# Angle tables of a state-space layer as products of two short tables, built for one pair of groups at a time

## The chip, the cores and the metric

The kernel runs on one core of one Trainium2 chip. The metric is the device time of one execution in microseconds. The three runs of the kernel before took 2749.91, 2758.4 and 2762.81 us, so its median is 2758.4 us.

## The reference

The program is one layer of a hybrid encoder over 2048 positions and 1024 channels. One normalized input h goes through one input projection whose columns feed three head groups: a diagonal complex state-space layer (S5), a differential attention and an HGRN2 gated recurrence. Their outputs go through one output projection and are added to the input; a gated MLP with a causal convolution and a last normalization follow. The change lies wholly in the first group:

```python
dt = exp(log_step)[:, None]
mag, ang = exp(lam_re * dt), lam_im * dt          # 16 groups x 64 states
lb = mag * (cos(ang) + i sin(ang))
bu[s] = B_bar @ u[s]                               # per group, 16 inputs
x[s]  = lb * x[s-1] + bu[s]                        # complex scan over 2048 positions
y     = Re(C @ x) + d * u
out   = gelu(y) * sigmoid(gelu(y) @ w_glu)
```

## The kernel before

`phase_s5` computes the layer with the 2048 positions cut into 256 chunks of T = 8. Inside a chunk the recurrence is folded into matrices (QP, QS, MG, C1, C2). Between chunks only the state after each chunk is scanned, 256 steps per group. To make that scan real, each state is turned back by its angle times the chunk number, scanned with the real factor `mag8`, and turned forward again. This takes a cosine and a sine table of 256 entries for each of the 16 groups on each of 128 partitions: the tiles `s_ct` and `s_sn`.

The phase has two parts, and both are Python generators whose `yield` marks where other work may be emitted between.

The parameter part (lines 383 to 552) runs beside the first normalization and projection (`phase_a`). It makes `E`, the sine and cosine of the angle times 8, 16, ... 1024 (line 478), QP and QS by rotations on VectorE (lines 516 to 519), and C1 and C2 by the same rotation on GpSimd, eight times six instructions (line 536, written in the body of the lambda at line 537). The rotations take their temporaries from the pool `s_e`, tags `t0` and `t1`, two buffers each. The pool is closed at line 553, and the pool `s_w` of the main part is opened after it on the same side of the memory.

The main part (lines 556 to 669) loops over four quarters `q` of four groups each. A quarter loads its inputs `U` by two DMAs on the queue of SyncE (line 560; the tile has two buffers). It then builds `CT` and `SN` for its four groups on GpSimd, one buffer each, by doubling: in step i the first n = 2^i columns, turned by E[i], give the next n columns, with six instructions a step (lines 577 to 584) and eight steps. Then come two pairs of groups. For a pair, ScalarE copies `s_un` out of U, TensorE transposes it (`s_pu`, line 594) and QP and QS (`s_pq`, line 604), TensorE multiplies (`s_pw`, line 617), VectorE multiplies the result by the two tables (`s_w`, lines 623 and 624), GpSimd adds (line 625), VectorE scans (`s_yy`, line 627), GpSimd multiplies by the two tables (`s_ya`, `s_yb`, lines 633 and 636), and TensorE sums three products (`s_py`, lines 646 to 651) for the gelu. The five PSUM tiles of this part share three buffers of one tag.

Beside the main part run the rest of the input projection (`a_p`) and the preparation of MLP weights (`f_sum`, `f_w`, `Wd`), which are the left side of a weave; the right side is S5, then HGRN2 (`phase_hgrn`), then output projection and MLP (`phase_tail`). After the projections the left side becomes the attention. The weave fixes the order in which work is emitted, by costs attached to the yields (6.0 for a projection step, 5.0 for an S5 step, 2.5 for an HGRN2 step). A planner then lists the instructions of each engine in a fixed order, and on the chip each engine runs its list in order and waits for what its next instruction needs.

Of the kernel before, what the change touches and what calls it, by code (L numbers as in the profile page):

```python
# [9 lines left out]
F32 = mybir.dt.float32  # L10
# [4 lines left out]
ALU = mybir.AluOpType  # L15
# [342 lines left out]
def phase_s5(K, Ud, lam_re, lam_im, log_step, b_re, b_im, c_re, c_im, d, w_glu, Yd):  # L358


    tc, nc = K.tc, K.nc
    G, N, P, T, C = 16, 64, 16, 8, 256
    V = nc.vector

    def b3(a, n):
        return a.rearrange("p (g o) -> p g o", o=1).to_broadcast([128, a.shape[1], n])

    with ExitStack() as es:
# [4 lines left out]
        with ExitStack() as e2:  # L373
            cp = e2.enter_context(tc.tile_pool(name="s_c", bufs=1, reuse_waits="tile", side="right"))
            e3 = ExitStack()
            wk = e3.enter_context(tc.tile_pool(name="s_e", bufs=2, reuse_waits="tile", side="right"))
# [10 lines left out]
            for i, dst in enumerate((re, im)):  # L387
# [8 lines left out]
                out=ls, in_=log_step[0].rearrange("(o g) -> o g", o=1).to_broadcast([128, G])  # L396
# [23 lines left out]
            def tt(o, a, b, op):  # L420
                V.tensor_tensor(out=o, in0=a, in1=b, op=op)
# [25 lines left out]
            c1 = 6.28125  # L447
# [90 lines left out]

            MG = cp.tile([128, T, G, P], F32, name="s_mg")
# [15 lines left out]
            wk = e2.enter_context(tc.tile_pool(name="s_w", bufs=2, reuse_waits="tile", side="right"))  # L555
            for q in range(4):
                gs = slice(4 * q, 4 * q + 4)
                U = wk.tile([128, 2, T, 64], F32, tag="u", name="s_u")
# [6 lines left out]
                CT = wk.tile([128, 4, C], F32, tag="ct", bufs=1, name="s_ct")  # L565
                SN = wk.tile([128, 4, C], F32, tag="sn", bufs=1, name="s_sn")
                nc.gpsimd.memset(CT[:, :, 0:1], 1.0)
                nc.gpsimd.memset(SN[:, :, 0:1], 0.0)
                for i in range(8):
                    n = 1 << i  # L570
                    sw, co = E[i]
                    sb, cb = b3(sw[:, gs], n), b3(co[:, gs], n)
                    a, b = CT[:, :, 0:n], SN[:, :, 0:n]
                    t0 = wk.tile([128, 4, 128], F32, tag="tb0", bufs=1, name="s_tb0")
                    t1 = wk.tile([128, 4, 128], F32, tag="tb1", bufs=1, name="s_tb1")
                    pt = nc.gpsimd.tensor_tensor
                    pt(out=t0[:, :, 0:n], in0=a, in1=cb, op=ALU.mult)
                    pt(out=t1[:, :, 0:n], in0=b, in1=sb, op=ALU.mult)
                    pt(out=CT[:, :, n:2 * n], in0=t0[:, :, 0:n], in1=t1[:, :, 0:n], op=ALU.subtract)
                    t0 = wk.tile([128, 4, 128], F32, tag="tb0", bufs=1, name="s_tb0")  # L580
                    t1 = wk.tile([128, 4, 128], F32, tag="tb1", bufs=1, name="s_tb1")
                    pt(out=t0[:, :, 0:n], in0=b, in1=cb, op=ALU.mult)
                    pt(out=t1[:, :, 0:n], in0=a, in1=sb, op=ALU.mult)
                    pt(out=SN[:, :, n:2 * n], in0=t0[:, :, 0:n], in1=t1[:, :, 0:n], op=ALU.add)
                yield 1
                for gg in range(0, 4, 2):
                    UG = wk.tile([128, 2, C], F32, tag="ug", name="s_ug")
# [24 lines left out]
                    for e in range(2):  # L612
                        g = 4 * q + gg + e
                        l = gg + e
                        pw = ps_p.tile([128, 2, C], F32, tag="s", name="s_pw")
                        for i in range(2):
# [6 lines left out]
                        tt(w0, pw[:, 0, :], CT[:, l, :], ALU.mult)  # L623
                        tt(w1, pw[:, 1, :], SN[:, l, :], ALU.mult)
# [9 lines left out]
                            out=YA[:, e, 1:C], in0=yy[:, 0:C - 1], in1=CT[:, l, 0:C - 1], op=ALU.mult  # L634
                        )
                        nc.gpsimd.tensor_tensor(
                            out=YB[:, e, 1:C], in0=yy[:, 0:C - 1], in1=SN[:, l, 0:C - 1], op=ALU.mult
# [1497 lines left out]
```

## Time and profile before

| | |
|---|---|
| median of three runs | 2758.4 us |
| profiled execution, device time | 2750.61 us |
| its span | 2748.9 us |
| TensorE busy | 2429.6 us (88%) |
| VectorE busy | 1924.5 us (70%) |
| GpSimd busy | 1357.3 us (49%) |
| granted TensorE clock, mean | 0.928 |

The span runs from the first to the last instruction of the profiled execution; the device time has 1.7 us around it. TensorE is the busiest engine, so a stretch in which it stands idle is the first place where time can be won. Busy shares of the whole say little of one stage: GpSimd is at 49% over the span, and far above that while S5 runs.

### The profile page before, as it was taken

The numbers are of one execution on the slowest core, as the hardware profiler recorded it, in microseconds if no ns is written. First come the engines' busy times: TensorE is split into PE (matmuls) and PEld (weight loads), VectorE is DVE, ScalarE is ACT, GpSimd is POOL, SyncE is SP. The second block draws the span as 40 slices with busy tenths as digits, with TensorE's granted clock in tenths as the row PEclk, the third lists the DMA queues.
The fourth block names the chain that finished last, engine by engine and source line by source line (L and its number), as shares of the span: only waits on it lengthen the run. The fifth ranks groups of instructions, "written<-read, shape, count | busy, mean of one in ns | idle before, by whom it ended". The sixth has DMA issues, their size and how long they took to land. (4 is left out here: it accounts for less than half of the span.)

```text
span 2748.9 us, 42509 instructions
## 1 busy us (share of the span) xinstructions
PE 2429.6 (88%) x15438; PEld 1365.9 (50%) x15438; DVE 1924.5 (70%) x3497; ACT 1255.9 (46%) x2270; POOL 1357.3 (49%) x1149
## 2 busy tenths in 40 slices
PE   5998888988988899759998888599989999999998
PEld 4655547767766665334443334244435444444444
DVE  7567746888888785698678998966464655455565
ACT  6333344666656453465446566533144433333221
POOL 5788602444534442267656866615232444444280
PEclk8999999999988878869999999799999999999999
DMA  7675555565665446655555566598785655554733
GB/s 242 234 222 196 172 159 120 117 139 121 112 142 126 92 116 180 165 132 146 180 174 150 168 165 173 185 285 260 256 285 184 219 158 150 162 157 138 282 97 123
DMA packets 556738, 473.06 MB, mean 172 GB/s; under 512 B 277296, under 2 KB 433264, under 8 KB 555504
## 3 DMA queue, kind: packets, MB, share of 16 engines
q1 hardware_dynamic: 534352, 429.97, 55.1%
q10 hardware_dynamic: 22176, 40.38, 4.0%
q8 instruction: 121, 1.98, 0.3%
q14 instruction: 89, 0.73, 0.1%
HBM read 290.35 MB, written 125.83 MB: 151 GB/s over the span
## 5 line engine op out<-in xcount | busy, mean ns | idle before, releaser
L96 PE MATMUL f_pm<-f_q,f_w 128*128 128x512 f16 x3696 | 839.2, 387 | 34.5 <-DVE f_u L1863 10.4
L96 PEld LDWEIGHTS <-f_w 128*128 128x128 f16 x3696 | 363.6, 99 | 502.7 <-issue 77.0
L1786 PE MATMUL f_pd<-f_dw,f_da 128*128 128x512 f16 x1848 | 411.0, 384 | 8.4 <-DVE f_r L1764 7.0
L891 POOL TENSOR_TENSOR t_sc<-t_sc 128x1024 f16<-128x1024 f32 (+7 forms) x144 | 256.8, 1796 | 274.4 <-ACT t_sc L890 247.1
L1786 PEld LDWEIGHTS <-f_da 128*128 128x128 f16 x1848 | 182.0, 99 | 231.5 <-issue 21.5
L848 ACT ACTIVATE t_sc<-t_sc,t_nm 128x128 f32<-128x128 f32 (+7 forms) x192 | 228.9, 1194 | 81.6 <-DVE t_nm L843 81.0
L832 PE MATMUL t_ps<-t_k,t_q 96*128 96x512 f16 (+2 forms) x480 | 168.9, 386 | 100.6 <-DVE t_mx L836 93.3
L836 DVE CUSTOM_DVE_ANT_0 t_sc<-t_ps,t_base,t_mx 128x512 f32<-128x512 f32 (+3 forms) x288 | 185.2, 644 | 24.7 <-PE t_ps L832 15.5
L61 DVE TENSOR_TENSOR f_a<-f_t,f_a 128x512 f16<-128x512 f32 x132 | 155.6, 1200 | 53.4 <-ACT f_a L55 53.0
L867 DVE SCALAR_TENSOR_TENSOR t_sc<-t_sc,t_a 128x1024 f32<-128x1024 f32 (+7 forms) x144 | 180.5, 1279 | 1.3
L96 PE MATMUL g_pv<-g_w,g_h 128*128 128x256 f16 x1152 | 154.3, 292 | 18.7 <-ACT g_w L55 11.8
L913 PEld LDWEIGHTS <-t_wt 128*128 128x128 f16 x2448 | 108.2, 104 | 110.2 <-DMA t_wt<-t_sc 49.2
L1863 POOL TENSOR_TENSOR f_t<-f_t,f_t 128x512 f32<-128x512 f32 x66 | 100.9, 1543 | 121.2 <-ACT f_a L55 109.8
L96 PE MATMUL g_pq<-g_h,g_w 128*128 128x256 f16 x1152 | 149.7, 288 | 10.4 <-DVE g_sg L1160 5.4
L913 PE MATMUL t_po<-t_v,t_wt 128*128 128x64 f16 x2448 | 121.5, 202 | 38.3 <-DMA t_wt<-t_sc 33.0
L1863 POOL TENSOR_TENSOR f_k<-f_k,f_k 128x512 f32<-128x512 f32 x88 | 124.7, 1417 | 59.3 <-ACT f_k L1895 26.0
L1617 DVE SCALAR_TENSOR_TENSOR f_t<-f_u,f_cw,f_t 128x1024 f32<-128x1024 f32 x88 | 125.5, 1426 | 32.5 <-ACT f_t L1615 31.7
L890 ACT CAST t_sc<-t_sc 128x1024 f16<-128x1024 f32 (+7 forms) x144 | 111.7, 792 | 77.9 <-DVE t_sc L867 73.6
L836 DVE CUSTOM_DVE_ANT_0 t_sc<-t_ps,t_base 128x512 f32<-128x512 f32 (+2 forms) x192 | 121.0, 633 | 34.8 <-PE t_ps L832 21.4
L96 PEld LDWEIGHTS <-g_h 128*128 128x128 f16 x1152 | 118.0, 104 | 50.6 <-issue 22.5
L55 ACT ACTIVATE f_a<-f_t 128x512 f16<-128x512 f32 x154 | 94.8, 627 | 96.4 <-DVE f_a L61 32.1
L55 ACT ACTIVATE f_w<-f_sum 128x512 f16<-128x512 f32 x110 | 69.1, 628 | 150.0 <-DVE f_sum L139 65.1
(335 smaller groups left out, 4490.0 us busy)
## 6 DMA issues: line engine op xcount, KB each, us to landing
f_w<-Wd SPq DMA_DIRECT2D x231, 256.0 KB, 3.0
Wd<-f_w SPq DMA_DIRECT2D x154, 256.0 KB, 2.1
Ad<-f_a ACTq DMA_DIRECT2D x154, 256.0 KB, 2.6
f_da<-Ad SPq DMA_DIRECT2D x42, 768.0 KB, 5.1
g_h<-Hd SPq DMA_DIRECT2D x24, 1024.0 KB, 6.7
f_dst<-in_w_down_dram SPq DMA_DIRECT2D x48, 512.0 KB, 4.6
o_wst<-in_w_out_dram SPq DMA_DIRECT2D x24, 512.0 KB, 5.5
f_wst<-in_w_gate_dram SPq DMA_DIRECT2D x22, 512.0 KB, 5.5
```

The lines of the kernel that those rows point to most:

```text
L55: nc.scalar.activation(out=hi, in_=src, func=AF.Copy, scale=scale)
L61: nc.vector.tensor_tensor(out=lo, in0=src, in1=hi, op=ALU.subtract)
L96: nc.tensor.matmul(out=out, lhsT=lhs(a, k), rhs=rhs(b, k), start=(n == 0), stop=(n == 3 * nk - 1))
L832: nc.tensor.matmul(out=ps[:, 0:k1 - k0], lhsT=qt[:, c, 128 * (i % 4):128 * (i % 4) + 128], rhs=H.k[:, c, k0:k1], start=True, stop=True,)
L836: V.tensor_tensor_reduce(out=sc[c][:, k0:k1], in0=ps[:, 0:k1 - k0], in1=bs[:, k0:k1], scale=1.0, scalar=-3e38 if j == 0 else mx[:, c, j - ...
L848: nc.scalar.activation(out=sc[c][:, 0:L], in_=sc[c][:, 0:L], func=AF.Exp, scale=SLOPES[h], bias=nm[:, c:c + 1], accum_out=H.la[:, c, n_:n_ ...
L867: V.scalar_tensor_tensor(out=sc[0][:, k0:k1], in0=sc[1][:, k0:k1], scalar=a[:, 1:2], in1=sc[0][:, k0:k1], op0=ALU.mult, op1=ALU.add,)
L891: nc.gpsimd.tensor_tensor(out=hl[:, LM + k0:LM + k1], in0=sc[0][:, k0:k1], in1=hl[:, k0:k1], op=ALU.subtract,)
L913: nc.tensor.matmul(out=po, lhsT=wt[:, w, b, :], rhs=vt[:, b, 64 * v:64 * v + 64], start=(b == 0 and w + v == 0), stop=(b == i and w == 1),)
L1617: V.scalar_tensor_tensor(out=t0, in0=u[:, c:n + c], scalar=cw[:, c, m:m + 1], in1=t0, op0=ALU.mult, op1=ALU.add,)
L1786: nc.tensor.matmul(out=ps[t], lhsT=a[:, q, x, tk], rhs=w[:, y, q, :], start=(first and q + x + y == 0), stop=(last and q == n - 1 and y == 1),
L1863: eng.tensor_tensor(out=o, in0=a, in1=b, op=op)
```

## The change

The short tables `FC` and `FS` are built once, in the parameter part: for each of the 16 groups, 16 cosines and sines of the angle times 0 to 15 (a = 0) and times 0, 16, ... 240 (a = 1). They are made by the same doubling, by VectorE, with four steps of six instructions for each a, and take their temporaries from the tags `t0` and `t1` of the pool `s_e`. A new `yield 1` stands ahead of this.

The full table of a pair of groups is then made by `table(g)`: 256 = 16 x 16 entries by the addition theorem, cos(x+y) and sin(x+y) from the two short tables, with six GpSimd instructions of 512 columns, whose factors are read with zero steps. The tile `s_ct` and the tile `s_sn` now hold two groups and have two buffers. `table(0)` is emitted ahead of the loop, and each pair emits the table of the next pair before its own work. `U` goes from two buffers to one.

```diff
+            yield 1
+            FC, FS = [cp.tile([128, 2, G, 16], F32, name=f"s_f{i}") for i in range(2)]
+            nc.gpsimd.memset(FC[:, :, :, 0:1], 1.0)
+            nc.gpsimd.memset(FS[:, :, :, 0:1], 0.0)
+            for a in range(2):
+                for i in range(4):
+                    n = 1 << i
+                    sw, co = E[4 * a + i]
+                    sb, cb = b3(sw, n), b3(co, n)
+                    c, s = FC[:, a, :, 0:n], FS[:, a, :, 0:n]
+                    t = [
+                        wk.tile([128, G, 8], F32, tag=f"t{j % 2}", name=f"s_t{j}")[:, :, 0:n]
+                        for j in range(4)
+                    ]
+                    tt(t[0], c, cb, ALU.mult)
+                    tt(t[1], s, sb, ALU.mult)
+                    tt(FC[:, a, :, n:2 * n], t[0], t[1], ALU.subtract)
+                    tt(t[2], s, cb, ALU.mult)
+                    tt(t[3], c, sb, ALU.mult)
+                    tt(FS[:, a, :, n:2 * n], t[2], t[3], ALU.add)
...
+            def table(g):
+                gs = slice(g, g + 2)
+                ct, sn = [
+                    wk.tile([128, 2, 16, 16], F32, tag=n, name="s_" + n) for n in ("ct", "sn")
+                ]
...
+                for eng, o, (a, b), (c, d), op, n in (
+                    (nc.gpsimd, ct, (c1, c0), (s1, s0), ALU.subtract, "tb0"),
+                    (nc.gpsimd, sn, (s1, c0), (c1, s0), ALU.add, "tb1"),
+                ):
+                    t = wk.tile([128, 2, 16, 16], F32, tag=n, bufs=1, name="s_" + n)
+                    eng.tensor_tensor(out=o, in0=a, in1=b, op=ALU.mult)
+                    eng.tensor_tensor(out=t, in0=c, in1=d, op=ALU.mult)
+                    eng.tensor_tensor(out=o, in0=o, in1=t, op=op)
+                return [o.rearrange("p g a b -> p g (a b)") for o in (ct, sn)]
+            ahead = table(0)
             for q in range(4):
-                gs = slice(4 * q, 4 * q + 4)
-                U = wk.tile([128, 2, T, 64], F32, tag="u", name="s_u")
+                U = wk.tile([128, 2, T, 64], F32, tag="u", bufs=1, name="s_u")
...
-                CT = wk.tile([128, 4, C], F32, tag="ct", bufs=1, name="s_ct")
-                SN = wk.tile([128, 4, C], F32, tag="sn", bufs=1, name="s_sn")
-                nc.gpsimd.memset(CT[:, :, 0:1], 1.0)
-                nc.gpsimd.memset(SN[:, :, 0:1], 0.0)
-                for i in range(8):
...
                 for gg in range(0, 4, 2):
+                    CT, SN = ahead
+                    if 4 * q + gg + 2 < G:
+                        ahead = table(4 * q + gg + 2)
...
-                        tt(w0, pw[:, 0, :], CT[:, l, :], ALU.mult)
-                        tt(w1, pw[:, 1, :], SN[:, l, :], ALU.mult)
+                        tt(w0, pw[:, 0, :], CT[:, e, :], ALU.mult)
+                        tt(w1, pw[:, 1, :], SN[:, e, :], ALU.mult)
```

## Rows read from the trace of the kernel before

**Rows 1.** The page: the span, and the busy time of each engine.

```profile
span 2748.9 us, 42509 instructions
PE 2429.6 (88%) x15438; PEld 1365.9 (50%) x15438; DVE 1924.5 (70%) x3497; ACT 1255.9 (46%) x2270; POOL 1357.3 (49%) x1149
```

**Rows 2.** Busy time by stage: the stretch, its length, then busy time and instructions of TensorE, its weight loads, VectorE, ScalarE and GpSimd, and last the granted clock, the DMA share and GB/s. The stretches are the parameter part's end, the four quarters of the main part, and the attention with what runs beside it.

```profile
98.00:147.00 49.00, 49.00 (x283) 27.57 (x282) 14.99 (x19) 10.17 (x19) 42.95 (x49) 1.00 0.68 243
147.00:195.00 48.00, 42.18 (x225) 26.02 (x223) 31.08 (x47) 18.72 (x37) 39.15 (x86) 0.93 0.82 233
195.00:243.00 48.00, 42.38 (x236) 27.14 (x235) 39.28 (x57) 19.27 (x39) 38.38 (x70) 0.93 0.64 202
243.00:291.00 48.00, 40.81 (x206) 23.49 (x205) 34.02 (x51) 15.93 (x31) 35.20 (x68) 0.96 0.55 187
291.00:345.00 54.00, 45.44 (x250) 28.30 (x248) 39.78 (x60) 18.55 (x34) 40.34 (x68) 0.91 0.56 179
...
700.00:1790.00 1090.00, 911.88 (x6494) 523.38 (x6495) 890.36 (x1642) 589.02 (x1026) 607.73 (x412) 0.88 0.57 151
```

**Rows 3.** What TensorE waited for from 147 to 345 us: total us, times, longest us.

```profile
PE s_pu L594 <- DVE s_w L421: 17.7, 3, 8.0
PE s_pu L594 <- ACT s_un L592: 4.0, 1, 4.0
PE s_py L647 <- POOL s_ya L633: 2.6, 4, 1.2
PE s_py L651 <- POOL s_yb L636: 2.2, 7, 0.6
```

**Rows 4.** TensorE's timeline: start, duration, instructions; in brackets the idle time before and what ended it.

```profile
189.44 0.60 PE L594 MATMUL s_pu<-ident,s_un 128*128 128x128 f32 x4
...
220.56 1.11 PE L594 MATMUL s_pu<-ident,s_un 128*128 128x128 f32 x4 [5.36 <-DVE s_w L421]
...
222.32 1.80 PE L96 MATMUL a_p<-a_w,a_h 128*128 128x384 f16 x5
...
230.92 3.74 PE L96 MATMUL a_p<-a_w,a_h 128*128 128x384 f16 x22
...
267.36 1.11 PE L594 MATMUL s_pu<-ident,s_un 128*128 128x128 f32 x4 [4.32 <-DVE s_w L421]
...
319.04 1.11 PE L594 MATMUL s_pu<-ident,s_un 128*128 128x128 f32 x4 [8.00 <-DVE s_w L421]
```

**Rows 5.** GpSimd's timeline: the last of the C1 and C2 rotations, the first instruction of each of the four tables, the last one of the first two, and the first pair's own instructions.

```profile
145.34 1.86 POOL L537 TENSOR_TENSOR s_c<-s_t,s_t 128x256 f32<-128x256 f32 x2
147.14 0.10 POOL L567 MEMSET s_ct<- 128x4 f32 x1
...
172.59 1.26 POOL L584 TENSOR_TENSOR s_sn<-s_tb,s_tb 128x512 f32<-128x512 f32 x1
174.39 1.41 POOL L625 TENSOR_TENSOR s_w<-s_w,s_w 128x256 f32<-128x256 f32 x2 [0.54 <-DVE s_w L421]
...
179.23 1.17 POOL L636 TENSOR_TENSOR s_yb<-s_yy,s_sn 128x255 f32<-128x255 f32 x1
...
191.06 0.10 POOL L567 MEMSET s_ct<- 128x4 f32 x1
...
218.03 1.59 POOL L584 TENSOR_TENSOR s_sn<-s_tb,s_tb 128x512 f32<-128x512 f32 x1
...
239.27 0.10 POOL L567 MEMSET s_ct<- 128x4 f32 x1
...
288.71 0.10 POOL L567 MEMSET s_ct<- 128x4 f32 x1
```

**Rows 6.** GpSimd's table instructions of 512 columns from 147 to 345 us, by form: count, busy us, mean ns, idle before.

```profile
L584 POOL TENSOR_TENSOR s_sn<-s_tb,s_tb 128x512 f32<-128x512 f32 x4 | 6.0, 1508 | 0.3
L579 POOL TENSOR_TENSOR s_ct<-s_tb,s_tb 128x512 f32<-128x512 f32 x4 | 5.4, 1346 | 0.3
L577 POOL TENSOR_TENSOR s_tb<-s_ct,s_col 128x512 f32<-128x512 f32 x4 | 4.9, 1214 | 0.3
...
L582 POOL TENSOR_TENSOR s_tb<-s_sn,s_col 128x512 f32<-128x512 f32 x4 | 4.2, 1040 | 0.3
```

**Rows 7.** VectorE instructions with two inputs in the parameter part: count, duration in ns (shortest, median, longest), first and last start, forms.

```profile
L421 DVE TENSOR_TENSOR s_col<-s_col,s_col x15: 162/169/1143, 34.8 to 60.3; 128x16 f32<-128x16 f32 x14, 128x144 f32<-128x144 f32 x1
L421 DVE TENSOR_TENSOR s_t<-s_qp,s_col x14: 409/412/1699, 66.0 to 91.9; 128x256 f32<-128x256 f32 x14
```

**Rows 8.** The loads of U: time from issue to landing; and what SyncE's queue waited for most from 100 to 420 us (total us, times, longest us).

```profile
DMA to landing us min/median/max: 3.6/4.7/6.0
```

```profile
SPq L143 <- DVE f_w L63: 101.5, 55, 6.9
```

**Rows 9.** The end of the projections and the start of HGRN2: the first load of its weights on SyncE's queue, what TensorE waited for from 380 to 440 us, and TensorE's rows of one projection group of HGRN2.

```profile
382.31 0.53 SPq L1121 DMA_DIRECT2D g_wst<-in_w_in_dram  x1
```

```profile
PE g_pv L96 <- ACT g_w L55: 7.7, 1, 7.7
...
PE g_pq L96 <- ACT g_w L55: 0.9, 1, 0.9
```

```profile
422.43 5.40 PE L96 MATMUL g_pq<-g_h,g_w 128*128 128x256 f16 x48
```

**Rows 10.** TensorE's longest wait in total, over the whole span: total us, times, longest us.

```profile
PE t_ps L832 <- DVE t_mx L836: 93.3, 69, 11.6
```

More of the change, by code (lines that the diff above doesn't have):

```diff
@@ L555, in phase_s5 @@
             wk = e2.enter_context(tc.tile_pool(name="s_w", bufs=2, reuse_waits="tile", side="right"))
+            def table(g):
[3 more added lines that the diff above has]
+                ]
+                c1, s1 = [
+                    f[:, 1, gs, :].rearrange("p g (a o) -> p g a o", o=1).to_broadcast([128, 2, 16, 16])
+                    for f in (FC, FS)
+                ]
+                c0, s0 = [
+                    f[:, 0, gs, :].rearrange("p g (o b) -> p g o b", o=1).to_broadcast([128, 2, 16, 16])
+                    for f in (FC, FS)
+                ]
+                for eng, o, (a, b), (c, d), op, n in (
[8 more added lines that the diff above has]
+            ahead = table(0)
             for q in range(4):
-                gs = slice(4 * q, 4 * q + 4)
-                U = wk.tile([128, 2, T, 64], F32, tag="u", name="s_u")
+                U = wk.tile([128, 2, T, 64], F32, tag="u", bufs=1, name="s_u")
                 for a in range(2):
@@ L564, in phase_s5 @@
                     )
-                CT = wk.tile([128, 4, C], F32, tag="ct", bufs=1, name="s_ct")
-                SN = wk.tile([128, 4, C], F32, tag="sn", bufs=1, name="s_sn")
-                nc.gpsimd.memset(CT[:, :, 0:1], 1.0)
-                nc.gpsimd.memset(SN[:, :, 0:1], 0.0)
-                for i in range(8):
[L570 to L584, printed above, removed]
                 yield 1
                 for gg in range(0, 4, 2):
+                    CT, SN = ahead
+                    if 4 * q + gg + 2 < G:
+                        ahead = table(4 * q + gg + 2)
                     UG = wk.tile([128, 2, C], F32, tag="ug", name="s_ug")
@@ L613, in phase_s5 @@
                         g = 4 * q + gg + e
-                        l = gg + e
                         pw = ps_p.tile([128, 2, C], F32, tag="s", name="s_pw")
@@ L633, in phase_s5 @@
                         nc.gpsimd.tensor_tensor(
-                            out=YA[:, e, 1:C], in0=yy[:, 0:C - 1], in1=CT[:, l, 0:C - 1], op=ALU.mult
+                            out=YA[:, e, 1:C], in0=yy[:, 0:C - 1], in1=CT[:, e, 0:C - 1], op=ALU.mult
                         )
                         nc.gpsimd.tensor_tensor(
-                            out=YB[:, e, 1:C], in0=yy[:, 0:C - 1], in1=SN[:, l, 0:C - 1], op=ALU.mult
+                            out=YB[:, e, 1:C], in0=yy[:, 0:C - 1], in1=SN[:, e, 0:C - 1], op=ALU.mult
                         )
```

## The prediction

> **What bounds the kernel now.** I read the page's busy times first. TensorE works 2429.6 of 2748.9 us [rows 1], so what counts is where it stands still or runs slowly, and whether S5 causes it.
>
> The second view is the busy time by stage. While the four quarters of S5's main part run, GpSimd is busy 35 to 40 us of each 48 (54 in the last), TensorE only 41 to 45, at a granted clock of 0.91 to 0.96; in the 49 us before it was busy throughout, at 1.00 [rows 2]. The reader is to see that the stage's pace is set by GpSimd and that TensorE loses time there.
>
> The third view says what TensorE waited for in these 198 us: 17.7 us, in three waits, for VectorE's `s_w` at the next `s_pu`; 4.0 us once for `s_un`; 4.8 us in eleven short waits for `s_ya` and `s_yb` [rows 3]. The name `s_w` is a middleman. In the timeline the three waits end at 220.56, 267.36 and 319.04 us [rows 4], and for the first of them GpSimd's timeline shows the last table instruction starting at 218.03 and lasting 1.59 us [rows 5]: VectorE cannot make `s_w` ahead of the table, its PSUM buffer stays taken, and the transposes of the next pair wait for the buffer. So the table of each new quarter stops TensorE once; only that of the first quarter does not.
>
> A stop costs more than its length. Four `s_pu` take 0.60 us undisturbed and 1.11 behind a stop; 22 `a_p` of one form take 3.74 us (0.17 each), and the five behind the first stop 1.80 instead of 0.85 [rows 4]. The granted clock says the same [rows 2]: behind a stop the engine runs for a while at 1.2 instead of 2.4 GHz.
>
> **The change part by part.**
>
> *The long tables go.* Each took 48 instructions. GpSimd's timeline has the first from 147.14 to 173.85 us and the second from 191.06 to 219.62 [rows 5], 26.7 and 28.6 us, a few of the pair's own memsets among them; four make about 110 us. The spacing of their starts is 44, 48 and 49 us, a whole quarter.
>
> *The pair tables come.* Six instructions of 512 columns, four products and two sums. Products of this size lasted 1.04 to 1.21 us in the mean, sums of two full tables 1.35 to 1.51 [rows 6], so a table takes 4 x 1.04 + 2 x 1.35 = 6.9 to 4 x 1.21 + 2 x 1.51 = 7.9 us. Products with both factors read by zero steps are not in the trace; I take the same prices, 7.4 us a table and 59 us for eight. GpSimd is rid of about 51 us. A pair's own GpSimd work runs from 174.39 to 180.40 us, 6 us [rows 5]. A pair then needs some 14 us of GpSimd, a quarter 28 in place of 44 to 49, and S5's main part can end up to 65 us earlier. The end of the kernel doesn't move by that: TensorE has the projections to do meanwhile, and only its own losses count.
>
> *What TensorE wins.* A table made one pair ahead is there when `s_w` needs it: 17.7 us of waits go. With them go the slow starts: by the rows, 0.5 us in `s_pu` and 0.95 in `a_p`, and as much again as the former for the `s_pq` between them that I don't show; I take 1.8 us a stop, 5.5 for three. From above, the clock rows of the last three quarters give 48 x 0.07 + 48 x 0.04 + 54 x 0.09 = 10.1 us [rows 2]. Late next are `s_ya` and `s_yb`.
>
> *What the order on GpSimd costs.* A pair table becomes possible when the pair before last has given its buffer back, that is right behind the last `s_yb`. It then stands in GpSimd's list ahead of line 625 of the next pair, whose scan, `s_ya`, `s_yb` and `s_py` all wait behind it. Bounds: nothing, if `s_w` comes later than the table ends; up to 7.4 us at each of seven pairs, 52 us, if TensorE's list holds nothing to fill in. The waits for `s_ya` and `s_yb` were 4.8 us before, with no table in front of most of them. I take their doubling, 4.8 us lost, because projections are there to fill and TensorE's list is planned with the tables in it.
>
> *The short tables* add 48 VectorE instructions of 16 to 128 columns and two memsets. The nearest rows are 0.16 to 0.17 us at 16 columns and 0.41 at 256 [rows 7], about 0.21 at the mean size here: 48 x 0.21 = 10 us. The longest of these forms took 1.14 and 1.70 us, so if half are stretched like that it is 40 us. They are emitted behind the rotations of C1 and C2, with which they share temporaries, and GpSimd ends these at 147.2 us [rows 5]. Ahead of that VectorE has room: busy 15 of 49 us from 98 to 147 [rows 2]. I cost them at nothing. If instead they wait for the rotations, the main part, whose pool opens only when that of the parameter part closes, starts 10 us later; TensorE has projections then, and the first `s_w` would still come no later, since the first table is 7 us and not 27. Without cover it is 10 us of TensorE.
>
> The trace has VectorE's `s_t` at 0.41 us in the median and 1.70 at worst, in a stretch with GpSimd at work [rows 7]. The Trainium skill, "SBUF — State Buffer", section "Who interferes with whom", says that a VectorE instruction with two SBUF inputs and a GpSimd instruction that reads SBUF shut each other out for the whole instruction. By that rule all 48 would be exposed beside the rotations, near the 40 us and not the 10; and 51 us less GpSimd work would in turn free VectorE in S5's stage. Both would fall in time that VectorE has over there, so the sum stays.
>
> *One buffer for U.* Before, the loads of later quarters ran far ahead. Now a quarter's load is issued after the last `s_un` of the quarter before, lands 4.7 us later (3.6 to 6.0), and may stand behind a write in SyncE's list that waits up to 6.9 us [rows 8]. Behind it in that list stand the weight loads and all writes of the projections. From the last `s_un` to the next one there is a pair's time, 14 us, against 1.5 + 4.7 + 6.9 = 13.1 at worst, so I cost it at nothing. Its other end: three stops like that of the first load, 4.0 us [rows 3] with 1.8 of slow start each, 17 us.
>
> The sum: 17.7 + 5.5 - 4.8 = 18.4 us won. The profiled execution took 2750.6 us (span 2748.9 and 1.7 around it); 2732.2 is 0.9933 of it. That execution lies 7.8 us under the median of the runs shown, 2758.4; by the same share the median becomes 2740.
>
> **The rivals** (times as medians).
>
> *More is won: the start of HGRN2 closes up too.* Its first weight load is issued at 382.31 us, as S5's memory comes free, and TensorE then waits 7.7 and 0.9 us for these weights as the projections run out [rows 9]. S5 ending 50 us earlier would load them beside projections. For it: the load sits right at S5's end. Against: the order of emission may hold HGRN2 back. It adds 8.6 and a slow start, some 10 us: 2730, and 2720 if the waits for `s_ya` vanish too.
>
> *The stops only change their name.* The three waits for tables become three waits for U's load, 17 us, or seven waits of 2.5 us behind a pair table. For it: SyncE's list is often held up [rows 8]. Against: slack of a pair's time. Then 17.7 + 5.5 - 4.8 - 17 = 1 us won: 2757.
>
> *Slower: HGRN2 overtakes the projections.* With S5 done early, TensorE takes HGRN2's groups (5.40 us for 48 matmuls [rows 9]) ahead of the last projections, and the attention, which needs these, starts later. From the emission costs, 12 projection steps are left when S5 is emitted, worth 28 of HGRN2's steps, and four of these are two groups: up to 14 groups, 75 us. The attention's stage has VectorE busy 890 of 1090 us [rows 2], and its exponent chain keeps TensorE waiting 93.3 us [rows 10]; work taken out from under it leaves TensorE idle there. If half of those 75 us are not won back, it is 38 - 18 = 20 us slower, 2778. The point: it decides if over 18 us of the delay reach the attention's end. For it: the attention chain is late in the run. Against: VectorE is not full there, and the tail can fill in.
>
> That the change doesn't do what it says would be seen as `s_w` still waiting for `s_ct`; with two buffers and the table emitted a pair ahead I see no ground for it.
>
> **How the numbers follow.** Forecast, 2740 (2728 to 2752): 0.42. More won, about 2725: 0.13. Stops renamed, about 2757: 0.25. Slower, about 2778: 0.20. The range from 2705 to 2779 takes in the further win, the clock's upper figure and half of the slow case. Half a per cent, 13.8 us, is about what a measurement of this kernel can tell from no change. Under 2744.6 lie 0.36 of the forecast's 0.42, the 0.13 and 0.02 of the third: 0.51. Above 2772.2 lie 0.15 of the slow case and 0.04 of the third: 0.19. Within: 0.30.
>
> **What would show it.** Right: no `s_w` waiting for `s_ct`, the three stops before `s_pu` gone, the clock near 1.00 from 195 us on, table instructions near 60 us in all, S5's last `s_yb` some 50 us earlier. Wrong in a step: `s_pu` waiting for `s_un` at each quarter (U), long waits of `s_py` (order on GpSimd), the main part starting after 155 us (short tables). The prediction fails if S5's stage is short of stops and the end still doesn't move; then I would look at where the attention starts.

## The result and the profile after

The changed kernel takes 2773.46 us (median of 15 runs, 2763.48 to 2782.38); the kernel before, run beside it, takes 2761.09 (15 runs, 2749.91 to 2768.82). The ratio is 1.005, with a 95% interval of 1.0037 to 1.0063: half a per cent slower, where 18 us of gain were forecast. The profiled execution took 2780.5 us (span 2778.7), at the upper end of its runs; the medians differ by 12.4 us, the two profiled executions by 30.

The page after, to be held against [rows 1]:

```profile
span 2778.7 us, 42387 instructions
PE 2422.5 (87%) x15438; PEld 1361.5 (49%) x15438; DVE 1940.4 (70%) x3545; ACT 1260.5 (45%) x2274; POOL 1312.5 (47%) x999
```

GpSimd is rid of 44.8 us (1357.3 to 1312.5), VectorE has 15.9 more. Next the busy time by stage of after, with the columns of [rows 2]:

```profile
98.00:147.00 49.00, 49.00 (x288) 28.64 (x286) 14.46 (x17) 11.05 (x19) 39.85 (x46) 0.99 0.67 236
147.00:195.00 48.00, 42.97 (x212) 22.18 (x209) 35.66 (x90) 16.15 (x31) 23.05 (x29) 0.96 0.82 250
195.00:243.00 48.00, 39.43 (x227) 26.70 (x227) 40.23 (x53) 18.65 (x38) 40.61 (x46) 0.96 0.54 167
243.00:291.00 48.00, 39.26 (x213) 24.50 (x214) 41.00 (x56) 17.42 (x34) 38.84 (x42) 1.00 0.61 197
291.00:345.00 54.00, 49.10 (x278) 29.46 (x277) 41.02 (x76) 27.43 (x45) 15.81 (x27) 1.00 0.58 186
```

The granted clock of the four stretches rose (0.93, 0.93, 0.96 and 0.91 before). But TensorE is busy 170.76 us of the 198, and was 170.81. Not one microsecond of its idle time went. What it waited for from 147 to 345 us in after (total us, times, longest us) says why:

```profile
PE s_py L674 <- DVE s_w L421: 7.7, 4, 2.9
PE s_py L675 <- POOL s_ya L661: 6.5, 7, 1.5
PE s_py L679 <- POOL s_yb L664: 4.8, 13, 0.6
PE s_pu L623 <- ACT s_un L621: 2.1, 1, 2.1
PE a_p L96 <- DVE a_vo L63: 1.9, 1, 1.9
PE s_py L674 <- DVE s_z L430: 1.9, 2, 1.6
```

The three stops of 17.7 us ahead of `s_pu` are gone, as forecast (0.4 us are left under that name). In their place stand short waits of `s_py`: 7.7 + 6.5 + 4.8 + 1.9 = 20.9 us, against 4.8 us in [rows 3]. All waits of the view add up to 26.9 us, those before to 27.1: the 26.5 of [rows 3] and one of 0.6 at `s_py` behind a table's memset, which the rows leave out.

Followed back, the new waits end at VectorE. It waited 13.0 us for the long table `s_ct` in before (first line below); in after it waits for GpSimd only once (second line), and GpSimd waits for it (third and fourth; all from 147 to 345 us):

```profile
DVE s_w L421 <- POOL s_ct L579: 13.0, 4, 5.3
```

```profile
DVE s_yy L655 <- POOL s_w L653: 1.0, 1, 1.0
```

```profile
POOL s_w L653 <- DVE s_w L421: 37.6, 10, 12.8
...
POOL s_ya L661 <- DVE s_yy L655: 7.3, 8, 1.7
```

The longest of the waits of `s_py` shows how, on TensorE, VectorE and GpSimd:

```profile
225.93 0.80 PE L674 MATMUL s_py<-s_mg,s_ug 128*128 128x128 f32 x2 [2.94 <-DVE s_w L421]
```

```profile
218.77 1.51 DVE L139 TENSOR_TENSOR f_sum<-f_wst 128x512 f32<-128x512 f32 x1 [2.19 <-DMA f_wst<-in_w_gate_dram]
...
225.47 0.41 DVE L421 TENSOR_TENSOR s_w<-s_pw,s_sn 128x256 f32<-128x256 f32 x1
```

```profile
225.95 1.41 POOL L653 TENSOR_TENSOR s_w<-s_w,s_w 128x256 f32<-128x256 f32 x2 [1.63 <-DVE s_w L421]
```

From 218.77 us on VectorE's list holds four instructions that prepare MLP weights (`f_sum`, `f_w`), one of them waiting for its DMA, then one of S5's gelu, and only then `s_w`. The product reads no `s_w`; what it can wait for is the PSUM buffer that VectorE gives back with it. Of the 20.9 us of `s_py`, in 26 waits, all but 0.95 us lead back to VectorE's list in this way. Two waits, the 0.95 us, lead on to a pair table that stands ahead of line 653 in GpSimd's list.

GpSimd's timeline of after shows the main part's start (start, duration; in brackets the idle time before):

```profile
147.75 2.37 POOL L537 TENSOR_TENSOR s_c<-s_t,s_t 128x256 f32<-128x256 f32 x2
166.01 1.05 POOL L597 TENSOR_TENSOR s_ct<-s_f 128x512 f32<-128x512 f32 x1 [15.89 <-issue]
```

The rotations end at 150.1 us, VectorE makes the short tables only then, GpSimd idles 15.9 us, and the first pair table begins at 166.0 instead of 147.1 us. GpSimd's table instructions of 512 columns from 147 to 345 us, by form (count, busy us, mean ns), answer to [rows 6]:

```profile
L599 POOL TENSOR_TENSOR s_sn<-s_sn,s_tb 128x512 f32<-128x512 f32 x8 | 12.3, 1544 | 0.0
L599 POOL TENSOR_TENSOR s_ct<-s_ct,s_tb 128x512 f32<-128x512 f32 x8 | 11.6, 1455 | 0.0
L598 POOL TENSOR_TENSOR s_tb<-s_f 128x512 f32<-128x512 f32 x8 | 11.2, 1398 | 0.2 <-DVE s_f L421 0.2
L597 POOL TENSOR_TENSOR s_sn<-s_f,s_f 128x512 f32<-128x512 f32 x8 | 10.6, 1330 | 0.0
L597 POOL TENSOR_TENSOR s_ct<-s_f 128x512 f32<-128x512 f32 x8 | 10.2, 1275 | 15.9 <-issue 15.9
L598 POOL TENSOR_TENSOR s_tb<-s_f,s_f 128x512 f32<-128x512 f32 x8 | 9.8, 1222 | 0.0
```

They sum to 65.7 us, 8.2 a table.

Behind S5 the view turns. TensorE's timeline of after at the end of the projections, to be read with [rows 9]:

```profile
378.08 4.44 PE L96 MATMUL g_pq<-g_h,g_w 128*128 128x256 f16 x24 [2.67 <-DMA g_h<-Hd]
...
427.20 5.42 PE L96 MATMUL g_pq<-g_h,g_w 128*128 128x256 f16 x48
...
433.80 3.10 PE L96 MATMUL a_p<-a_w,a_h 128*128 128x384 f16 x18
...
457.05 0.40 PE L860 MATMUL t_ps<-t_k,t_q 96*128 96x128 f16 x3
```

HGRN2's groups start 16 us earlier than before (378.1, before 394.3) and stand between the last projections, which end 29 us later; the attention's first product comes at 457.05 us (420.7 before). That is what the prediction's slower rival described. TensorE's longest wait of the whole span, that of `t_ps` for `t_mx`, is nearly what it was: 96.4 us, 93.3 in [rows 10].

The attention's last product (`t_po`, 2448 matmuls; first and last start) in before and in after:

```profile
L913 PE MATMUL t_po<-t_v,t_wt x2448: 189/193/261, 438.0 to 1941.2; 128*128 128x64 f16 x189
```

```profile
L941 PE MATMUL t_po<-t_v,t_wt x2448: 189/193/261, 474.3 to 1966.7; 128*128 128x64 f16 x189
```

From there to the end of the span it is 807.7 us before and 812.0 after. So of the 30 us between the profiled executions 25.5 arise before the attention ends.

### The profile page after: what moved, and what is told of

It reads as the page before. It is cut to its first block, busy times and chain, and to the rows that moved or that the text cites. A ratio compares the mean times of both kernels' runs of the same rounds, so it can differ in the third digit from the quotient of the medians.

```text
span 2778.7 us, 42387 instructions
## 1 busy us (share of the span) xinstructions
PE 2422.5 (87%) x15438; PEld 1361.5 (49%) x15438; DVE 1940.4 (70%) x3545; ACT 1260.5 (45%) x2274; POOL 1312.5 (47%) x999
## 4 chain that ended last, share of the span: by engine, by line
PE 34%; DVE 21%; issue 10%; DMA 9%; ACT 8%; POOL 6%; SPq 1%; ACTq 0%; DVEq 0%; POOLq 0%
PE f_pm L96 13%; PE f_pd L1814 9%; DVE t_sc L864 4%; DMA f_dst<-in_w_down_dram 3%; ACT t_sc L876 3%; DVE t_sc L895 2%; DMA t_wt<-t_sc 2%; PE g_pq L96 2%; PE o_pe L1439 2%; DVE f_t L1645 1%; DVE f_w L63 1%; PE o_pm L1521 1%; PE g_pv L96 1%; DVE f_a L61 1%; POOL f_dst L1891 1%
## 5 line engine op out<-in xcount | busy, mean ns | idle before, releaser
L96 PE MATMUL f_pm<-f_q,f_w 128*128 128x512 f16 x3696 | 830.6, 384 | 42.1 <-ACT f_part L1606 10.6
L860 PE MATMUL t_ps<-t_k,t_q 96*128 96x512 f16 (+2 forms) x480 | 165.3, 375 | 107.2 <-DVE t_mx L864 96.4
L895 DVE SCALAR_TENSOR_TENSOR t_sc<-t_sc,t_a 128x1024 f32<-128x1024 f32 (+7 forms) x144 | 166.4, 1181 | 1.1
L96 PE MATMUL g_pq<-g_h,g_w 128*128 128x256 f16 x1152 | 155.4, 294 | 13.1 <-DVE g_sg L1188 10.3
L96 PEld LDWEIGHTS <-g_w 128*128 128x128 f16 x1152 | 118.8, 105 | 46.3 <-issue 20.0
```

Of the source, the lines that this page charges most:

```text
L96: nc.tensor.matmul(out=out, lhsT=lhs(a, k), rhs=rhs(b, k), start=(n == 0), stop=(n == 3 * nk - 1))
L860: nc.tensor.matmul(out=ps[:, 0:k1 - k0], lhsT=qt[:, c, 128 * (i % 4):128 * (i % 4) + 128], rhs=H.k[:, c, k0:k1], start=True, stop=True,)
L895: V.scalar_tensor_tensor(out=sc[0][:, k0:k1], in0=sc[1][:, k0:k1], scalar=a[:, 1:2], in1=sc[0][:, k0:k1], op0=ALU.mult, op1=ALU.add,)
```

## The experiments

The theories that the expectations name are these. A: HGRN2's groups ahead of the projections delay the attention, and that is the loss. B: the late short tables (main part at 166 us) are. E: the single buffer for U is. C: the order of the attention's stage is merely reshuffled; D widens it. D: any edit of S5 gives all work planned behind it another order, the kernel before has a good one, and the loss is in that order. D' is D's statement on S5's own stage: when S5 starts does not matter there. Each kernel was timed beside the kernel before in its own group of runs, whose median was 2758.2 to 2761.9 us; the ratios are against that.

**e1 and e2: HGRN2 held.** In after, HGRN2 is emitted only when the last projection step is; e2 also lets 28 of its steps go first, at no cost.

```diff
+        emitted = []
...
             for _ in first:
                 yield LW[0]
+            emitted.append(1)
...
             for _ in s5:
                 yield LW[2]
+            while not emitted:
+                next(fore)
+            yield None
```

> The changed kernel, but HGRN2 is emitted only when the last projection step has been emitted, and the weave's accounts are set equal there. Theory A (with S5's tables early, HGRN2's first groups are taken ahead of the last projections, and the attention that needs these starts 36 us later, 457 instead of 421 us): last a_vo back to 405 to 415 us, first t_ps near 420 us, time 2745 to 2762. Theory B (the loss is S5's own late start, 166 instead of 147 us, because the short tables wait for the rotations): last a_vo stays about 25 us late or the time stays at 2770 to 2778. Theory C (the order of the attention stage is merely reshuffled): no relation, anywhere from 2755 to 2785.

> As e1_hold, but the 28 HGRN2 steps that the costs would have put beside the last projections are emitted at once behind them, ahead of the attention. Theory A: the projections end as early as in e1_hold, the attention starts up to 20 us later than there since HGRN2 has the first call; time between 2750 and 2773. If HGRN2's lag in e1_hold does harm, this one is the faster of the two by 5 us or more. Theory B: 2770 to 2778. Theory C: no relation.

e1 takes 2763.94 us, ratio 1.0006 (0.9992 to 1.002); e2 2765.01, ratio 1.0005 (0.9992 to 1.0019). The attention starts at 413.2 and 414.5 us. Both give the loss back (e1 2 us past what A had said), which fits A, and C and D as well, since both also reorder everything behind. All engines and SyncE's queue keep after's list up to some 330 us, and no instruction of the change is touched: so the loss of after is in the order of what follows, whichever feature of it counts.

**e3: the short tables' temporaries in slots of their own.**

```diff
-                        wk.tile([128, G, 8], F32, tag=f"t{j % 2}", name=f"s_t{j}")[:, :, 0:n]
+                        wk.tile([128, G, 8], F32, tag=f"f{j % 2}", bufs=1, name=f"s_t{j}")[:, :, 0:n]
```

> The changed kernel, but the short tables take their temporaries from tags of their own, so that they need not wait for GpSimd's rotations of C1 and C2. Both theories: the short tables are ready before 147 us and the first pair table starts near 150 instead of 166 us. Theory A: S5 ends 10 to 15 us earlier still, HGRN2 overtakes as before or more, first t_ps at 450 us or later, time 2768 to 2785. Theory B: time back to 2750 to 2762.

2772.73 us, ratio 1.0032 (1.0019 to 1.0045). The main part's first copy out of U comes 17 us earlier than in after (159.8, after 176.9) and nothing that can be told is won, which speaks against B. It isn't a test of the earlier start alone: TensorE's list differs from after's from 61 us on. And A is weakened: the attention starts still later (475.7 us), yet its last product comes 13 us earlier than after's:

```profile
L941 PE MATMUL t_po<-t_v,t_wt x2448: 189/193/261, 488.4 to 1953.9; 128*128 128x64 f16 x189
```

**e4: the kernel before with one buffer for U.**

```diff
-                U = wk.tile([128, 2, T, 64], F32, tag="u", name="s_u")
+                U = wk.tile([128, 2, T, 64], F32, tag="u", bufs=1, name="s_u")
```

> The kernel before with one thing of the change: one buffer for U. If the single buffer by itself costs (loads held up on SyncE's queue), there are waits of s_un for U at each quarter and the time goes up by 5 us or more; theories A and B: no such waits of TensorE beyond the first quarter's, 2755 to 2766.

2774.61 us, ratio 1.0038 (1.0026 to 1.005). None of the long tables is touched, the projections end where they did (last `a_vo` at 408.7 us, 408.9 before), and the kernel loses about as much as by the whole change. Neither A nor B explains that; D and E came from here. TensorE's list differs from 164 us on, and 88% of its matmuls keep their place. After with two buffers for U was not tried.

**e5: a harmless edit.** Four added memsets of 0.10 us each, which write what is already there.

```diff
                 nc.gpsimd.memset(CT[:, :, 0:1], 1.0)
+                nc.gpsimd.memset(CT[:, :, 0:1], 1.0)
```

> The kernel before, with the small memset of the table's first column issued twice: four instructions of a fraction of a microsecond each on GpSimd, which compute nothing new. They change the order that the planner gives to the work from the second half of S5 on (about a quarter of TensorE's instructions come at another place). Theory D (the order of everything behind S5 is reshuffled by any edit of S5, and the kernel before has a lucky one): 2766 to 2775 us, as with the single U buffer. Theory E (the single buffer for U itself costs something): 2758 to 2765.

2787.67 us, ratio 1.0105 (1.0092 to 1.0119): 28 us slower, twice the loss of the change and more than D had said. S5's stage and the projections stay where they were (last `a_vo` at 407.5 us), the attention starts at 423.2, and still it ends late:

```profile
L914 PE MATMUL t_po<-t_v,t_wt x2448: 189/193/261, 429.8 to 1976.4; 128*128 128x64 f16 x189
```

Of TensorE's 15,438 matmuls about three quarters stand at the same place in its list as before. The other quarter is interleaved in another way: 77 places in S5's stage, from 179 us on, and the rest between 345 and 1500 us. The busy time by stage shows where that begins to tell, first before, then e5 (columns as in [rows 2]):

```profile
413.00:500.00 87.00, 80.50 (x782) 66.82 (x781) 56.72 (x172) 39.48 (x96) 27.20 (x30) 0.94 0.54 116
500.00:700.00 200.00, 174.81 (x1841) 139.64 (x1840) 176.20 (x503) 134.36 (x344) 93.06 (x83) 0.91 0.59 126
```

```profile
413.00:500.00 87.00, 68.67 (x603) 55.33 (x604) 60.62 (x183) 42.50 (x107) 26.94 (x28) 0.80 0.57 119
500.00:700.00 200.00, 171.80 (x1743) 137.03 (x1742) 154.42 (x427) 116.22 (x296) 93.95 (x80) 0.89 0.50 113
```

From 413 to 700 us, where HGRN2 and the attention run side by side, TensorE does 14.8 us less and VectorE 17.9 us less in the same time, and the granted clock of the first stretch is 0.80 instead of 0.94.

**e6, e7, e8: the hold elsewhere.** The edit of e1 in the kernel before, in e4, and together with e3's.

> The kernel before, with HGRN2 held until the last projection step is emitted. Theory A (what costs is HGRN2's steps ahead of the projections, and the change lets in more of them): in the kernel before few are ahead, so 2756 to 2765. Theory D (any reshuffling of the order costs): 2766 to 2775. If the hold is a gain of its own, whatever stands ahead of it: 2745 to 2755, and then e1 shows nothing about the change.

> The kernel before with a single buffer for U (which took 2774.6 us) and HGRN2 held as in e1. Theory A/D (the loss of the single buffer is in the order of the steps behind S5): the hold gives it back, 2758 to 2766. Theory E (the buffer itself costs, in S5's stage): it stays at 2770 to 2778.

> The kernel after with both edits: HGRN2 held as in e1 (2763.9 us) and the short tables' temporaries in slots of their own as in e3, by which S5's main part starts 12 us earlier. Theory A (the loss is HGRN2's overtaking alone, and S5 is not on the path that sets the end once HGRN2 is held): 2758 to 2766, no better than e1. Theory B (S5's late start costs): 2750 to 2756, faster than both kernels.

e6: 2767.18 us, ratio 1.0035 (1.0021 to 1.0049). e7: 2770.39, 1.0047 (1.003 to 1.0065). e8: 2780.77, 1.0073 (1.0058 to 1.0089). The hold costs in the kernel before, changes nothing that can be told in e4, and e8, which has e1's hold and e3's edit, is slower than either. A as a cause that a hold takes away falls with e7 and e8, which it had at 2766 at most; e8 misses B's number too, and e7's falls into E's, which e15 below excludes. D shared A's number for e7 and missed it as well: it says that an order can cost, not which one will. For e6 D's number was 2766 to 2775, A's 2756 to 2765; its median lies in the first.

**e9, e10, e11: a barrier.** A barrier of all engines behind S5 and the projections, in before, in after and in e5. Behind it the lists of the three kernels agree on every engine.

```diff
             while not emitted:
                 next(fore)
+            tc.strict_bb_all_engine_barrier()
             yield None
```

> The kernel before with a barrier of all engines behind S5 and the projections, ahead of HGRN2 and the attention. It is the base for e10 and e11: behind the barrier all three have the same order of instructions on every engine, so a difference between them can come only from what lies ahead of it. The barrier itself lets all engines run dry once: an estimate of 5 to 40 us on top of e6's 2767.

> The kernel after with the barrier of e9. Theory D (the change's own work costs and wins next to nothing, and what it lost is the order of the work behind S5): within 6 us of e9, and if anything below it by the 2 to 5 us by which the projections end earlier in e1 than in e6. Theory B (the change's own work, the late short tables and the single U, costs): 8 to 15 us above e9.

> The kernel of e5 (before with a small memset issued twice, 28 us slower than before) with the barrier of e9. Theory D (those 28 us are the order behind S5, which the barrier now keeps as in e9): within 3 us of e9. If a memset of 0.1 us did cost something where it stands: up to 28 us above e9.

e9 takes 2790.76 us, ratio 1.0113 (1.009 to 1.0136); e10 2795.9, 1.0129 (1.0107 to 1.0151); e11 2791.86, 1.0115 (1.0091 to 1.0139). With the order behind S5 made equal, e5's 28 us shrink to 1.1, which can't be told from nothing. That is the plainest evidence for D. The change stands 5.1 us above its base, but the intervals overlap in most of their width, so the sign of its own work isn't settled here. The first product behind the barrier in e9, e10 and e11, on TensorE's timeline:

```profile
413.74 0.59 PE L832 MATMUL t_ps<-t_k,t_q 96*128 96x128 f16 x3 [13.61 <-SPq L2068]
```

```profile
414.58 0.58 PE L860 MATMUL t_ps<-t_k,t_q 96*128 96x128 f16 x3 [13.73 <-SPq L2096]
```

```profile
409.85 0.59 PE L833 MATMUL t_ps<-t_k,t_q 96*128 96x128 f16 x3 [13.62 <-SPq L2069]
```

e9 and e10 arrive within 0.9 us of each other.

**e12: added work in an unchanged order.** The memset of `MG` (line 540) a second time.

```diff
             nc.gpsimd.memset(MG, 0.0)
+            nc.gpsimd.memset(MG, 0.0)
```

> The kernel before with another memset issued twice, that of the block table at the start (1.8 us of GpSimd, four times the work that e5 added in all); here the planner leaves the order of every engine as it was, but for the one added instruction. Theory D (what costs is a changed order, not added work): 2756 to 2765, as before. If added GpSimd work costs by itself: 2770 and more.

2757.8 us, ratio 0.9999 (0.9987 to 1.0011). Four times e5's added work, at the start of the kernel (4.2 us), no change of order, no loss. The attention ends as before:

```profile
L914 PE MATMUL t_po<-t_v,t_wt x2448: 189/193/261, 439.7 to 1944.0; 128*128 128x64 f16 x189
```

**e13 to e16: the kernels ended after S5 and the projections.** Both sides of the weave return there (the first is ahead of the attention's pool `t_c`, the second ahead of HGRN2), and a few rows of `Yd` go out.

```diff
             for _ in first:
                 yield LW[0]
+            return
...
             for _ in s5:
                 yield LW[2]
+            return
```

> The kernel before, ended after S5 and the projections: HGRN2, the attention and all behind them are left out, and the output holds only a few rows of S5's result. Up to where HGRN2 begins the order on every engine is that of before. The base for e14 to e16; an estimate of 400 to 440 us from the last projection at about 400 us in e9 and e11.

> The kernel after, cut as e13. Theory D (the stops that went on TensorE came back as small waits, so the change's own work neither wins nor costs): within 3 us of e13. As the prediction had it (18.4 us of TensorE's time won in this stage): 13 to 20 us below e13. Theory B (the late short tables cost): 5 to 12 us above.

> The kernel before with a single buffer for U, cut as e13. Theory D (the 13 us that it cost uncut were the order behind S5): within 3 us of e13. Theory E (the buffer itself costs): 5 us and more above e13.

> The kernel after with the short tables' temporaries in slots of their own, cut as e13: S5's main part starts earlier. If the 19 us by which the main part starts later than before are what eats the gain: 8 to 15 us below e14. Theory D' (S5 runs beside the projections, and TensorE's own work and its small waits set the end whenever S5 starts): within 4 us of e14.

e13: 407.02 us (406.34 to 409.19). e14: 403.65 (401.62 to 405.48). e15: 408.21 (405.82 to 411.46). e16: 413.71 (412.4 to 415.32). As shares of the full kernel before they are 0.1476 (0.1471 to 0.1481), 0.1461 (0.1456 to 0.1465), 0.148 (0.1472 to 0.1488) and 0.1499 (0.1494 to 0.1505). So the change, in the order that it gets in this stage (TensorE's list is another from 158 us on), wins 3.4 us up to the end of the projections, a small gain clear of the noise, just past what D had allowed (3 us) and a fifth of what I had forecast. The single buffer for U costs nothing that can be told, so E falls; B, which had e14 5 to 12 us above e13, falls with e14. The stage of e14 shows the same exchange as in after (TensorE's waits from 98 us to the end):

```profile
PE s_py L674 <- DVE s_w L421: 6.5, 3, 2.9
PE s_py L675 <- POOL s_ya L661: 6.2, 7, 1.4
PE s_pw L645 <- ACT s_qw L637: 4.1, 3, 2.0
PE s_py L679 <- POOL s_yb L664: 4.0, 11, 0.6
```

e13 has 17.9 us for `s_w` at `s_pu` in their place. e16 contradicts all that was said of it: S5 starts earlier (first `s_pu` at 159.2 us, 178.2 in e14), and the whole is 10 us longer. The windows of e14, then of e16, show where TensorE falls behind:

```profile
0.00:98.00 98.00, 65.75 (x445) 51.03 (x446) 77.28 (x225) 56.73 (x88) 54.94 (x48) 0.89 0.69 226
98.00:147.00 49.00, 49.00 (x263) 28.99 (x261) 13.74 (x17) 10.76 (x18) 39.19 (x45) 0.90 0.66 232
147.00:195.00 48.00, 44.85 (x237) 23.79 (x234) 35.87 (x90) 16.33 (x31) 23.73 (x29) 1.00 0.80 246
```

```profile
0.00:98.00 98.00, 62.55 (x410) 47.53 (x410) 79.83 (x254) 53.38 (x84) 54.38 (x44) 0.86 0.67 220
98.00:147.00 49.00, 45.43 (x268) 27.96 (x268) 17.85 (x32) 11.85 (x19) 39.98 (x47) 0.93 0.66 228
147.00:195.00 48.00, 39.94 (x214) 24.50 (x213) 38.16 (x47) 18.04 (x37) 43.31 (x49) 0.94 0.68 214
```

By 195 us e16 has done 53 matmuls fewer (892 against 945), and 35 of them are missing at 98 us, ahead of S5's main part. In e16 the short tables run on VectorE from 55.8 to 105.8 us, beside the first normalization, and TensorE's list is another from 61 us on. So e16, like e3, moves more than the start of S5, and which part of it costs the 10 us isn't shown.

**e17 and e18: after in two other orders.** Only the prices by which the weave emits the steps are changed: HGRN2's from 2.5 to 2.7, or the attention's from 0.44 to 0.42.

```diff
-LW = [6.0, 0.44, 5.0, 2.5, 0.72, 1.0]
+LW = [6.0, 0.44, 5.0, 2.7, 0.72, 1.0]
```

> The kernel after with HGRN2's steps counted at 2.7 in place of 2.5, so that in the emitted order more of the attention stands ahead of each HGRN2 step (VectorE has 80 attention steps ahead of HGRN2's tenth projection, 73 in after). Nothing else is changed. If the loss of after is its interleaving: the attention's last product comes before 1955 us and the time is 2750 to 2766. If some 10 us stay with the changed kernel whatever the order: 2768 to 2780.

> The kernel after with the attention's steps counted at 0.42 in place of 0.44: a change of the emitted order that is smaller ahead of 700 us than e17's (72 attention steps ahead of HGRN2's tenth projection, 73 in after). If the loss is the interleaving in that stage: 2765 to 2778, near after, whose interleaving it nearly keeps. If any change of the order scatters the time: anywhere from 2755 to 2790.

e17: 2767.53 us, ratio 1.0035 (1.0022 to 1.0049). e18: 2764.9, ratio 1.0026 (1.0014 to 1.0037). Neither reaches before. e18 lies under after (its interval ends at 1.0037, where after's begins); e17's interval overlaps after's. e17's time falls between its two expectations, though its attention ends at 1907.2 us, 34 us earlier than before's: the attention's end alone does not set the time when it comes early. e18 still gained at least as much (just under the 2765 that was said for that case), though all engines and SyncE's queue keep after's list up to 498 us, HGRN2's groups ahead of the last projections with it (last `a_vo` at 435.9 us, first `t_ps` at 454.6). From 413 to 700 us the windows of after, then of e18, are:

```profile
413.00:700.00 287.00, 250.60 (x2506) 201.68 (x2505) 222.14 (x635) 161.47 (x414) 123.95 (x112) 0.89 0.50 113
```

```profile
413.00:700.00 287.00, 257.62 (x2541) 206.22 (x2539) 227.74 (x655) 167.78 (x425) 128.79 (x114) 0.89 0.51 115
```

In these executions TensorE does 7.0 us more in e18 and VectorE 5.6. So about half of after's loss is in the order behind 498 us, with A's delay of the attention left as it was. It is not settled which feature of an order decides. No version beats the kernel before.

## Why the prediction was wrong

**The stage.** *What TensorE wins* was right in its event: the three stops went, 17.7 us to 0.4, the clock rose, and no `s_w` kept a new quarter's `s_pu` waiting. The step that failed is *What the order on GpSimd costs*: "their doubling, 4.8 us lost". In size: the waits of `s_py` rose by 15.5 us (5.4 to 20.9, with the 0.6 that [rows 3] leave out), and 3.1 us of other new waits came (`a_p`, `s_pz` and `s_pw`), against 18.8 us less at `s_pu`.

In its ground: a pair table ahead of the next pair in GpSimd's list is behind 0.95 us of the 20.9; the rest is VectorE, for which the sum has no term. The prediction had GpSimd setting the stage's pace and left it so once GpSimd was relieved; it saw work on VectorE fall "in time that VectorE has over there". With the tables early, VectorE is busy 157.9 of the 198 us (144.2 before), S5's steps stand in its list between the preparations of MLP weights, and GpSimd and TensorE wait for it. This is read from the trace; no run took those preparations out of the stage. "Late next are `s_ya` and `s_yb`" named only a part: they rose by 6.5 us, and 9.6 us are `s_w` and `s_z` at the head of the same sum. From the first table to the last `s_yb` the main part takes 155.2 us (166.0 to 321.2) for 191.3 before, 19.4 us a pair where 14 of GpSimd had been reckoned, and TensorE now waits a little for each pair where it had waited long for each quarter. The rival "the stops only change their name" had this with the wrong heirs, U's load or the pair tables. In all 3.4 of the 18.4 us were won, by e14.

**The end.** The second failing step is one that isn't in the sum at all: that 18.4 us won in one stage are won at the end, "by the same share". The medians lie 12.4 us apart the wrong way, so behind the 3.4 us won some 16 were lost. e5, e11 and e12 show that a changed order behind S5 can cost 28 us with four memsets of 0.10 us added, that this goes when the order is made equal, and that more work without a change of order costs nothing. e1, e2, e17 and e18 have the change's work in other orders at ratios from 1.0005 to 1.0035; e3 and e8, which move the tables' temporaries as well, at 1.0032 and 1.0073. In e1 and e2 the lists are after's own up to some 330 us, in e18 up to 498 us, and they give back some 10, 9 and 6 of after's 12.4 us (medians, each against its own before). So nearly all of after's loss is in the order of what stands behind S5, and not in the changed work. Open are which feature of an order decides, why before's order is better than most that were tried, and what the changed work is worth at the end with the order behind it equal (3.4 us won by e14, nothing that can be told by e10).

**The slower rival.** "HGRN2 overtakes the projections" gave 2778 and a delay of the attention, and both look right: 2773 and 36 us. As the whole cause it does not hold. e18 keeps the delay (36 us in after, 34 in e18) and loses about half as much. e3 starts the attention 19 us later still and ends it 13 us earlier; e17 starts it at 455.2 us and ends it 59 us earlier than after; e5 starts it 2.5 us later than before and is the slowest of all without a barrier. A number that comes out near does not confirm its mechanism.

**The smaller steps.** GpSimd's relief: 44.8 us for the 51 said, since a table costs 8.2 us and not 7.4. *Short tables*: 48 instructions on VectorE are 9.3 us busy in after, 10 was said; the fear that they wait for the rotations came true (166 us, past the 155 named), and as priced it isn't seen as idle time: TensorE is busy 42.97 us from 147 to 195 us, 42.18 before. What the tables cost at an earlier place isn't separated (e16). *One buffer for U*: nothing, 2.1 us of waiting where 4.0 were before, though its loads took up to 9.2 us to land (6.0 in [rows 8]); the "13.1 at worst" had been summed with the median landing, and with 6.0 it is 14.4, past the pair's 14. The last `s_yb` came 17 us earlier, not 50. *More is won*: HGRN2's first weight load did come earlier, at 366.4 us (382.31 in [rows 9]), and the wait for these weights fell from 8.6 to 3.7 us, of which nothing is seen at the end.

In e16 the short tables run beside GpSimd's preparation of projection weights (`a_wst`, `a_w`) and its first rotations, and the 48 instructions are busy 21.5 us, 9.3 in after. 32 of them overlap a GpSimd instruction: 15 of these take 0.30 us or more, the longest 2.13 and 2.15, and 17 at most 0.28; the 16 that overlap none take at most 0.29. In after the only two over 0.29 us, 0.71 and 0.94, are those beside GpSimd's last rotation and its first pair table. The Trainium skill, "SBUF — State Buffer", section "Who interferes with whom", has a VectorE instruction with two SBUF inputs and a GpSimd instruction that reads SBUF shut each other out for the whole instruction. The long ones agree with that, all of them beside GpSimd; the 17 say that not every overlap shows.

## What to carry to other kernels

Where a planner lists the instructions, an edit is priced twice: by its own work, and by the new order of all that is planned behind it; here the first won 3 us and the second cost up to 28. Measure the two apart: a harmless edit that reorders, one that doesn't, a barrier that makes the order behind equal, and the kernel ended after the changed stage. And when a stop goes, sum the waits of the whole stage before and after: these were 27.1 and 26.9 us, so the stop had only been cut in pieces. Before relieving one engine, ask of each other one in the stage how near its limit it is; here VectorE was next and had no term in the sum.

## What was not expected of the hardware

GpSimd's products with both factors read by zero steps are dearer in the mean than those of the long tables, 1222 to 1398 ns against 1040 to 1214 [rows 6], but not because of the zero steps. They come at two levels, and the level goes with what VectorE runs as they begin:

```profile
215.50 1.07 DVE L63 SCALAR_TENSOR_TENSOR f_w<-f_sum,f_w 128x512 f16<-128x512 f32 x1 [0.74 <-ACT f_w L55]
```

```profile
215.99 1.50 POOL L597 TENSOR_TENSOR s_ct<-s_f 128x512 f32<-128x512 f32 x1
217.45 1.05 POOL L597 TENSOR_TENSOR s_sn<-s_f,s_f 128x512 f32<-128x512 f32 x1
```

Of the 32 products of after from 147 to 345 us, the 18 that begin while a weight preparation (`f_w`, `f_sum`) runs on VectorE take 1.38 to 1.50 us, three that begin beside the gelu's line 427 take 1.12 to 1.23, and the other 11 take 1.05. In before 4 of 16 begin beside such a preparation and take 1.37 to 1.49 us, the other 12 take 1.03 to 1.04. So reading with zero steps costs about 0.01 us, and the dearer mean comes from more of them beginning beside VectorE's preparations. The other way round, one of VectorE's `f_w` takes 1.54 us at 221.88 us, beside a pair table, and 0.68 at 156.68, with GpSimd idle. Nor was it expected that e16, with an earlier start of S5, is 10 us longer.
